# One level of Strassen's seven half-size products for the second product of each feed-forward sublayer

## The chip, the cores and the metric

The kernel runs on one core of a Trainium2 chip. The metric is the device time of one execution in microseconds. TensorE (PE) multiplies matrices and writes PSUM, of which this kernel uses eight banks of 128 x 512 float32; VectorE (DVE) and ScalarE (ACT) work elementwise between PSUM and the on-chip memory SBUF; SyncE (SP) issues the DMA transfers from the chip's main memory.

## The reference

Two layers, each of three sublayers: a half-step SwiGLU feed-forward, a token mixer (mLSTM in the first layer, Mamba-2 in the second), and another feed-forward. There are 512 tokens, 1024 model columns and 2816 feed-forward columns, all float32. So the feed-forward occurs four times:

```python
def swiglu(h, w1, w3, w2):
    return (jax.nn.silu(h @ w1) * (h @ w3)) @ w2

def sublayer(x, fn, g_pre, g_post, shift, scale, gate, weight):
    hmod = rms_norm(x, g_pre) * (1 + scale[:, None, :]) + shift[:, None, :]
    y = rms_norm(fn(hmod), g_post)
    return x + weight * gate[:, None, :] * y
```

The shift, scale and gate rows come from a product of the conditioning vector with the weights `ada_w` (adaLN). The change touches the product with `w2`: 512 x 2816 by 2816 x 1024.

## The kernel before

Every large product is made from split operands: a value becomes a high part in the type fp32r (a ScalarE copy) and a low part (VectorE: value minus high part). `mm3` (L171 to L175) then issues three matmuls for one block: high by high, high by low, low by high. Weights come through `unit` (L146): one 512 KB load into one of four `raw` buffers, a ScalarE copy to `wh` (L161) and a VectorE subtraction to `wl` (L162), three buffers each.

A feed-forward sublayer (`Ffn`) runs in two stages. In the first, `tile_in` makes 22 tiles `f` of 128 feed-forward columns by 512 tokens: two projections of 24 matmuls (w1, w3) into two of four rotating `mm` banks, Silu on ScalarE, the multiply on VectorE (L585), and a split into the halves `gh` and `gl`, which are kept for all 22 tiles. Between tiles `pump` adds steps of the adaLN product of later sublayers: a 512 KB load and a VectorE multiply-add (L195) each, and at the end of each such product a few small matmuls into an `aux` bank. The first four tiles are made in two halves of 256 tokens (`first`), since the second half of the tokens is normalised later.

In the second stage `out_proj` multiplies the tokens (stationary, 128 at a time) by blocks of `w2` (moving, 512 columns). The left half of the model columns is made first into four `aux` banks, then the right half into four `mm` banks; for the last five weight units of the right half, `out_tail` holds the weights and finishes one 128-token tile after another. For each finished bank `Post.evac` squares (ScalarE, L444) and multiplies by the gate row (VectorE, L445); `Post.finish` computes the norm and updates `x`, and `Pre.tok` and `Pre.half` normalise and transpose the tokens for the next sublayer, two 128-token tiles at a time, into eight chunks `hm` (L345 to L347).

SBUF tiles come from pools and from 52 numbered slots; a tile program orders the instructions of each engine ahead of time by priority, in which the program's order counts, and `tc.high_priority()` moves the split of weights up.

## Time and profile before

| | before |
|---|---|
| median of 3 runs | 2109.82 us (2108.58 to 2111.18) |
| the profiled execution | 2108.79 us, of which the profile's span is 2107.0 |
| TensorE busy | 2080.6 us, 99% of the span, 10686 matmuls |
| VectorE busy | 1256.6 us, 60% |
| ScalarE busy | 863.6 us, 41% |
| moved by DMA | 288.32 MB, 137 GB/s on average |

Busy times are shares of an average over stages. Matmuls are pipelined, so the durations of single matmuls overlap and their spacing in the timeline is what counts.

### The profile page before, as it was taken

What the parts mean: (1) busy time and instruction counts of PE and PEld (TensorE: products, weight loads), DVE (VectorE), ACT (ScalarE), POOL (GpSimd) and SP (SyncE); (2) the same over time, 40 slices, a digit from 0 to 9 for tenths busy, and PEclk for the clock granted to TensorE, in tenths of its full rate; (3) what the DMA queues carried; (4) which work ended last, traced back from release to release, by engine and by line L of the source; (5) the groups of instructions that cost most, each with busy time, mean ns of one, the idle gap of its engine ahead of it and who ended that gap; (6) DMA issues with size and microseconds to landing.
All of it is one profiled execution on the core that took longest, in us unless ns stands there. A gap on an engine that the chain in (4) does not pass through costs nothing.

```text
span 2107.0 us, 27076 instructions
## 1 busy us (share of the span) xinstructions
PE 2080.6 (99%) x10686; PEld 1749.8 (83%) x10686; DVE 1256.6 (60%) x1935; ACT 863.6 (41%) x1401; POOL 12.6 (1%) x33
## 2 busy tenths in 40 slices
PE   7999999999999999999999999999999999999998
PEld 5888888988789888888988888898788789888887
DVE  8977524658886667236565423679898865333333
ACT  5433323545463333235332223554656645222231
POOL 0000000000000000000000000000000000000000
PEclk9999999999999999999999999999999999999999
DMA  7566534145325776342565234233434332333331
GB/s 273 189 210 220 189 99 141 51 136 174 122 88 183 230 238 222 99 128 92 171 219 181 90 100 128 93 95 104 140 99 128 110 100 81 100 92 99 100 102 59
DMA packets 89966, 288.32 MB, mean 137 GB/s; under 512 B 11432, under 2 KB 11432, under 8 KB 89840
## 3 DMA queue, kind: packets, MB, share of 16 engines
q1 hardware_dynamic: 89840, 286.61, 42.6%
q8 instruction: 83, 1.36, 0.3%
q14 instruction: 43, 0.35, 0.0%
HBM read 284.32 MB, written 2.24 MB: 136 GB/s over the span
## 4 chain that ended last, share of the span: by engine, by line
PE 93%; DVE 3%; ACT 2%; DMA 1%; issue 1%; SPq 0%; DVEq 0%; ACTq 0%
PE mm L173 25%; PE mm L175 25%; PE mm L174 25%; PE aux L173 4%; PE aux L174 4%; PE aux L175 4%; PE aux L332 1%; PE aux L976 1%; PE aux L753 1%; DMA raw<-in_ada_w 1%; DVE wl L162 1%; PE aux L987 1%; PE aux L941 1%; PE aux L739 0%; ACT wh L161 0%
## 5 line engine op out<-in xcount | busy, mean ns | idle before, releaser
L173 PE MATMUL mm<-hm,wh 128*128 128x512 f32 (+1 forms) x2128 | 770.9, 364 | 1.2 <-ACT hm L417 1.1
L175 PE MATMUL mm<-hm,wl 128*128 128x512 f32 (+1 forms) x2128 | 768.7, 362 | 0.0
L174 PE MATMUL mm<-hm,wh 128*128 128x512 f32 (+1 forms) x2128 | 768.3, 362 | 0.0
L161 ACT ACTIVATE wh<-raw 128x1024 fp32r<-128x1024 f32 (+1 forms) x402 | 373.1, 943 | 740.2 <-PE mm L174 268.5
L162 DVE TENSOR_TENSOR wl<-raw,wh 128x1024 fp32r<-128x1024 f32 (+1 forms) x402 | 428.5, 1078 | 400.7 <-ACT wh L161 392.3
L173 PEld LDWEIGHTS mm<-hm,wh 128*128 128x128 f32 x2128 | 400.9, 189 | 63.4 <-issue 2.1
L175 PEld LDWEIGHTS mm<-hm,wl 128*128 128x128 f32 x2128 | 402.0, 189 | 61.8 <-issue 1.1
L174 PEld LDWEIGHTS mm<-hm,wh 128*128 128x128 f32 x2128 | 401.9, 189 | 60.5 <-issue 1.4
L195 DVE SCALAR_TENSOR_TENSOR acc<-raw,csil,acc 128x1024 f32<-128x1024 f32 x112 | 143.7, 1283 | 143.4 <-DMA raw<-in_ada_w 142.7
L585 DVE TENSOR_TENSOR s<-s,mm 128x512 f32<-128x512 f32 (+1 forms) x97 | 59.9, 618 | 134.4 <-PE mm L175 134.3
L173 PE MATMUL mm<-wh,gh 128*128 128x512 f32 x352 | 137.5, 391 | 0.0
L175 PE MATMUL mm<-wh,gl 128*128 128x512 f32 x352 | 137.0, 389 | 0.0
L174 PE MATMUL mm<-wl,gh 128*128 128x512 f32 x352 | 137.0, 389 | 0.0
L173 PE MATMUL aux<-wh,gh 128*128 128x512 f32 x352 | 136.9, 389 | 0.0
L174 PE MATMUL aux<-wl,gh 128*128 128x512 f32 x352 | 136.9, 389 | 0.0
L175 PE MATMUL aux<-wh,gl 128*128 128x512 f32 x352 | 136.9, 389 | 0.0
L178 ACT ACTIVATE gh<-s 128x512 fp32r<-128x512 f32 (+1 forms) x100 | 57.8, 580 | 121.6 <-DVE s L585 112.9
L175 PEld LDWEIGHTS mm<-wh,gl 128*128 128x128 f32 x352 | 66.1, 188 | 13.9
L175 PEld LDWEIGHTS aux<-wh,gl 128*128 128x128 f32 x352 | 66.1, 188 | 13.8
L173 PEld LDWEIGHTS aux<-wh,gh 128*128 128x128 f32 x352 | 66.1, 188 | 13.8
L174 PEld LDWEIGHTS aux<-wl,gh 128*128 128x128 f32 x352 | 66.1, 188 | 13.6
L173 PEld LDWEIGHTS mm<-wh,gh 128*128 128x128 f32 x352 | 66.1, 188 | 13.5
(261 smaller groups left out, 2113.9 us busy)
## 6 DMA issues: line engine op xcount, KB each, us to landing
raw<-in_w SPq DMA_DIRECT2D x258, 512.0 KB, 3.7
raw<-in_ada_w SPq DMA_DIRECT2D x128, 512.0 KB, 4.3
raw<-in_mb_wx SPq DMA_DIRECT2D x24, 512.0 KB, 3.7
a<-in_ada SPq DMA_DIRECT2D x32, 256.0 KB, 5.4
raw<-in_mb_wz SPq DMA_DIRECT2D x16, 512.0 KB, 3.7
bc<-mb_a SPq DMA_DIRECT2D x32, 256.0 KB, 3.4
raw<-in_mb_wout SPq DMA_DIRECT2D x16, 512.0 KB, 3.7
raw<-in_ml_wkq SPq DMA_DIRECT2D x8, 512.0 KB, 3.7
```

Of the source, the lines that this page charges most:

```text
L161: act(hi[:, :b - a], raw[:, a:b], AF.Copy)
L162: tt(lo[:, :b - a], raw[:, a:b], hi[:, :b - a].bitcast(F32), ALU.subtract)
L173: matmul(ps, stat[0], mov[0], start=first, stop=False)
L174: matmul(ps, stat[0], mov[1], start=False, stop=False)
L175: matmul(ps, stat[1], mov[0], start=False, stop=last)
L178: act(dst_h, src, AF.Copy)
L195: stt(st["acc"], raw, csil[:, kc:kc + 1], st["acc"], ALU.mult, ALU.add)
L332: nc.tensor.transpose(self.pt[d // 2][:, o:o + P], scr[:, d * P:(d + 1) * P], ident)
L585: tt(s[:, a:b], s[:, a:b], p[1][:, a:b], ALU.mult)
L753: matmul(num[j][:, c * P:], vt[c // 2][:, o:o + P], st[c][:, c * P:], start=c == 0, stop=c == 3)
L941: matmul(ps, bt[:, c * P:(c + 1) * P], w, start=True, stop=True)
L976: return matmul(yp[e * 64:(e + 1) * 64, c * P:(c + 1) * P], xdt[c][:, hh * 64:(hh + 1) * 64], ws[e][:, c * P:(c + 1) * P], start=True, sto ...
```

## The change

The product with `w2` is cut into two by two blocks: tokens in halves of 256, the 22 feed-forward tiles in pairs (even, odd), model columns in halves of 512. Seven products of sums and differences of these blocks take the place of eight. `factors` makes the token side of a pair: sums on VectorE, then splits; three factors (products 1, 6, 7) live in buffers of the pool `yg` and are used at once, four (products 2 to 5) are kept in slots. `flush` loads both column halves of the pair's weights, adds them up, splits, and multiplies products 1, 7 and 6 between the tiles of the first stage. They accumulate in all four `aux` banks and two `mm` banks, so that the tiles of the first stage have two `mm` banks (`mm_turn`), and adaLN's small matmuls take a matmul bank where no other is free (`ps_ada`). In `outp`, products 5, 3, 4 and 2 follow, each with loads of its own; product 2 runs with product 4 for four of the 11 pairs, and for the other seven (`HELD`) from held weights at the end, one 128-token tile after another. The output blocks are sums of the seven, made in `yg` on VectorE; the first two token tiles are finished after product 4, the other two after product 2.

```diff
-W2_TAIL = 5
+HELD = 7
...
-    mm = pool("mm", 4, space=bass.MemoryType.PSUM)
+    mm = pool("mm", space=bass.MemoryType.PSUM)
...
-    def ps_mm():
-        return mm.tile([P, T], F32, tag="mm", name="mm")
+    mm_turn, mm_next = [0, 1, 2, 3], [0]
+    def ps_mm(k=None):
+        if k is None:
+            k = mm_turn[mm_next[0] % len(mm_turn)]
+            mm_next[0] += 1
+        return mm.tile([P, T], F32, tag=f"mm{k}", name="mm")
     def ps_aux():
         return banks.get(F32, "aux")
     done_ps = banks.free
+    def ps_ada():
+        if banks.free_:
+            ps = ps_aux()
+            return ps, lambda: done_ps(ps)
+        return ps_mm(), lambda: None
...
-            ps = ps_aux()
+            ps, done = ps_ada()
...
-            done_ps(ps)
+            done()
...
-    def pump(n):
-        settle()
+    def pump(n, ended=True):
+        if ended:
+            settle()
...
     class Ffn:
         def __init__(self, l, h):
-            self.l, self.h, self.s = l, h, 2 * h
-            self.g, self.w, self.raw = {}, {}, {}
+            self.l, self.h, self.sub = l, h, 2 * h
+            self.w, self.raw, self.s, self.half = {}, {}, {}, {}
+            self.kept, self.pairs, self.pending, self.m, self.n_done = {}, [], [], None, 0
         def weights(self, f, hold=False):
             self.w[f] = [unit(i["w13"][self.l, self.h, f, q], hold=hold, soon=not hold) for q in range(2)]
@@ -565,29 +580,111 @@
             if q == 0:
                 act(s0, s0, AF.Silu, bias=b)
                 return
-            self.g[f] = gh, gl = slot(F32R, "gh"), slot(F32R, "gl")
             stt(s0, s1, b, s0, ALU.add, ALU.mult)
-            split(gh, gl, s0)
-            free(s0, s1)
-
-        def tile_in(self, f, sl, hm, p=None):
+            free(s1)
+            self.gated(f, s0)
+        def tile_in(self, f, sl, hm, p=None, go=True):
             a, b = sl
             if f not in self.w:
                 self.weights(f)
             p = p or [ps_mm(), ps_mm()]
             for q in range(2):
                 proj(p[q], self.w[f][q], hm, sl)
-            if f not in self.g:
-                self.g[f] = (slot(F32R, "gh"), slot(F32R, "gl"))
-            gh, gl = self.g[f]
-            s = slot(name="s")
+            if f not in self.half:
+                self.half[f] = slot(name="s")
+            s = self.half[f]
             act(s[:, a:b], p[0][:, a:b], AF.Silu)
             tt(s[:, a:b], s[:, a:b], p[1][:, a:b], ALU.mult)
-            split(gh[:, a:b], gl[:, a:b], s[:, a:b])
-            free(s)
             if b == T:
                 for w in self.w[f]:
                     free(*w.tiles)
+                del self.half[f]
+                self.gated(f, s)
+                if go:
+                    self.step()
+        def gated(self, f, s):
+            self.s[f] = s
+            if f ^ 1 in self.s:
+                self.pairs.append(f // 2)
+        def step(self):
+            self.flush()
+            if self.pairs:
+                self.factors(self.pairs.pop(0))
+        def factors(self, j):
+            s0, s1 = self.s.pop(2 * j), self.s.pop(2 * j + 1)
+            H = T // 2
+            lo, hi = slice(0, H), slice(H, T)
+            raw = ygp.tile([P, D], F32, tag="yg", name="traw")
+            tt(raw[:, :T], s0, s1, ALU.add)
+            tt(raw[:, T:T + H], s0[:, lo], s1[:, hi], ALU.add)
+            tt(s0[:, hi], s0[:, hi], s0[:, lo], ALU.subtract)
+            tt(s1[:, lo], s1[:, lo], s1[:, hi], ALU.subtract)
+            th = ygp.tile([P, D], F32R, tag="yg", name="th")
+            tl = ygp.tile([P, D], F32R, tag="yg", name="tl")
+            early = {}
+            for n, (m, src) in enumerate(((1, raw[:, T:T + H]), (6, s0[:, hi]), (7, s1[:, lo]))):
+                c = slice(n * H, n * H + H)
+                split(th[:, c], tl[:, c], src)
+                early[m] = th[:, c], tl[:, c]
+            self.kept[j] = kept = {}
+            for (ma, a), (mb, b) in (((5, raw[:, lo]), (3, s0[:, lo])), ((2, raw[:, hi]), (4, s1[:, hi]))):
+                kh, kl = slot(F32R, "kh"), slot(F32R, "kl")
+                split(kh[:, lo], kl[:, lo], a)
+                split(kh[:, hi], kl[:, hi], b)
+                kept[ma], kept[mb] = (kh[:, lo], kl[:, lo]), (kh[:, hi], kl[:, hi])
+                kept[f"{ma}{mb}"] = kh, kl
+            free(s0, s1)
+            self.pending.append((j, early))
+        def product(self, ps, a, b, first, last):
+            for t in range(2):
+                c = slice(t * P, (t + 1) * P)
+                mm3(ps[t], (a[0][:, c], a[1][:, c]), b, first, last)
+        def w2(self, c, j):
+            raw = rawp.tile([P, 1024], F32, tag="raw", name="raw")
+            nc.sync.dma_start(raw, i["w2"][self.l, self.h, c, j])
+            return raw
+        def halves(self, raw, n=2 * T):
+            wh = whp.tile([P, 1024], F32R, tag="wh", name="wh")
+            wl = wlp.tile([P, 1024], F32R, tag="wl", name="wl")
+            split(wh[:, :n], wl[:, :n], raw[:, :n])
+            return [(wh[:, k * T:k * T + T], wl[:, k * T:k * T + T]) for k in range(n // T)]
+        def flush(self):
+            while self.pending:
+                j, a = self.pending.pop(0)
+                if self.m is None:
+                    self.m = {1: [ps_aux(), ps_aux()], 6: [ps_aux(), ps_aux()], 7: [ps_mm(2), ps_mm(3)]}
+                settle()
+                r0, r1 = self.w2(0, j), self.w2(1, j)
+                with tc.high_priority():
+                    tt(r1[:, :T], r1[:, :T], r0[:, :T], ALU.add)
+                    two = r0.rearrange("p (a b) -> p a b", b=T)
+                    tt(two, two, r1[:, T:].unsqueeze(1).to_broadcast([P, 2, T]), ALU.add)
+                    b1, b7 = self.halves(r0)
+                    b6, = self.halves(r1, T)
+                n = self.n_done
+                self.n_done += 1
+                for m, b in ((1, b1), (7, b7), (6, b6)):
+                    self.product(self.m[m], a[m], b, n == 0, n == NF // 2 - 1)
         def first(self, hm):
             for f in range(F_STAG):
@@ -595,16 +692,99 @@
             for f in range(F_STAG):
                 self.tile_in(f, HA, hm)
             for f in range(F_STAG):
-                self.tile_in(f, HB, hm)
+                self.tile_in(f, HB, hm, go=False)
+            mm_turn[:] = [0, 1]
         def rest(self, hm, start, rate):
             for f in range(start, NF):
                 self.tile_in(f, FULL, hm)
                 if f < ADA_END:
-                    pump(int((f - start + 1) * rate) - int((f - start) * rate))
-
-        def outp(self, post):
-            out_proj(i["w2"][self.l, self.h], [self.g[f] for f in range(NF)], W2_TAIL, post)
+                    pump(int((f - start + 1) * rate) - int((f - start) * rate), False)
+        def outp(self, nxt):
+            n = NF // 2
+            m5 = [ps_mm(0), ps_mm(1)]
+            def five(j):
+                raw = rawp.tile([P, 1024], F32, tag="raw", name="raw")
+                nc.sync.dma_start(raw[:, :T], i["w2"][self.l, self.h, 1, j, :, T:])
+                with tc.high_priority():
+                    b5, = self.halves(raw, T)
+                self.product(m5, self.kept[j][5], b5, j == 0, j == n - 1)
+            for j in range(n - 2):
+                five(j)
+            while self.pairs or self.pending:
+                self.step()
+            post = Post(self.l, self.sub, nxt)
+            m, yg = self.m, post.yg
+            lo, hi = slice(0, T), slice(T, D)
+            for t in range(2):
+                act(yg[2 + t][:, hi], m[1][t], AF.Copy)
+                tt(yg[t][:, lo], yg[2 + t][:, hi], m[7][t], ALU.add)
+                tt(yg[2 + t][:, hi], yg[2 + t][:, hi], m[6][t], ALU.add)
+            done_ps(*m[1], *m[6])
+            for j in range(n - 2, n):
+                five(j)
+            m3 = [ps_aux(), ps_aux()]
+            for j in range(n):
+                raw = self.w2(1, j)
+                with tc.high_priority():
+                    tt(raw[:, lo], raw[:, lo], raw[:, hi], ALU.subtract)
+                    b3, = self.halves(raw, T)
+                self.product(m3, self.kept[j][3], b3, j == 0, j == n - 1)
+                free(*self.kept[j]["53"])
+            for t in range(2):
+                act(yg[t][:, hi], m5[t], AF.Copy)
+                tt(yg[t][:, lo], yg[t][:, lo], m5[t], ALU.subtract)
+                tt(yg[t][:, hi], yg[t][:, hi], m3[t], ALU.add)
+                tt(yg[2 + t][:, hi], yg[2 + t][:, hi], m3[t], ALU.add)
+                post.evac(t, 1, yg[t][:, hi])
+            done_ps(*m3)
+            m4, m2 = [ps_aux(), ps_aux()], [ps_mm(2), ps_mm(3)]
+            held = {}
+            joint = range(3, 3 + 2 * (n - HELD), 2)
+            hs = [j for j in range(n) if j not in joint]
+            for j in range(n):
+                raw = self.w2(0, j)
+                k = self.kept[j]
+                if j in joint:
+                    with tc.high_priority():
+                        tt(raw[:, hi], raw[:, hi], raw[:, lo], ALU.subtract)
+                        b2, b4 = self.halves(raw)
+                    self.product(m4, k[4], b4, j == 0, j == n - 1)
+                    self.product(m2, k[2], b2, j == joint[0], False)
+                    free(*k["24"])
+                    continue
+                tt(raw[:, hi], raw[:, hi], raw[:, lo], ALU.subtract)
+                b4 = slot(F32R, "bh"), slot(F32R, "bl")
+                split(*b4, raw[:, hi])
+                held[j] = slot(F32R, "bh"), slot(F32R, "bl")
+                split(*held[j], raw[:, lo])
+                self.product(m4, k[4], b4, j == 0, j == n - 1)
+                free(*b4)
+            for t in range(2):
+                tt(yg[t][:, lo], yg[t][:, lo], m4[t], ALU.add)
+                act(yg[2 + t][:, lo], m4[t], AF.Copy)
+            done_ps(*m4)
+            for t in range(2):
+                post.evac(t, 0, yg[t][:, lo])
+                post.finish(t)
+            for t in range(2):
+                c = slice(t * P, (t + 1) * P)
+                for j in hs:
+                    ah, al = self.kept[j][2]
+                    mm3(m2[t], (ah[:, c], al[:, c]), held[j], False, j == hs[-1])
+                    if t:
+                        free(*self.kept[j]["24"], *held[j])
+                u = 2 + t
+                tt(yg[u][:, lo], yg[u][:, lo], m2[t], ALU.add)
+                post.evac(u, 0, yg[u][:, lo])
+                tt(yg[u][:, hi], yg[u][:, hi], m2[t], ALU.subtract)
+                post.evac(u, 1, yg[u][:, hi])
+                post.finish(u)
+            mm_turn[:] = [0, 1, 2, 3]
+            return post
...
     for f in range(3, START_L + 6):
-        f00.tile_in(f, FULL, p.hm)
+        f00.tile_in(f, FULL, p.hm, go=False)
         k = f - START_L
         if k >= 0:
             f00.late(k // 2, k % 2, early[k // 2][k % 2])
         pump(START_R[f - 3])
     done_ps(mod0)
+    mm_turn[:] = [0, 1]
     f00.rest(p.hm, START_L + 6, ADA_R[0])
-    post = Post(0, 0, (0, 1))
-    f00.outp(post)
+    post = f00.outp((0, 1))
...
-    post = Post(0, 2, (1, 0))
-    f01.outp(post)
+    post = f01.outp((1, 0))
...
-    f11.outp(Post(1, 2))
+    f11.outp(None)
```

## Rows read from the trace of the kernel before

**Rows 1.** The page's head: span, and busy time (share of the span) by engine.

```profile
span 2107.0 us, 27076 instructions
PE 2080.6 (99%) x10686; PEld 1749.8 (83%) x10686; DVE 1256.6 (60%) x1935; ACT 863.6 (41%) x1401; POOL 12.6 (1%) x33
```

**Rows 2.** The chain of work that ended last, shares of the span by engine.

```profile
PE 93%; DVE 3%; ACT 2%; DMA 1%; issue 1%; SPq 0%; DVEq 0%; ACTq 0%
```

**Rows 3.** Waits: engine, line, releaser: us in total, times, longest.

```profile
DVE acc L195 <- DMA raw<-in_ada_w: 142.7, 65, 5.1
...
PE aux L410 <- DVE diag L392: 12.3, 4, 9.8
PE aux L941 <- DVE xw L938: 1.3, 1, 1.3
```

**Rows 4.** Groups of instructions by line and shape: count, busy us, mean ns.

```profile
L162 DVE TENSOR_TENSOR wl<-raw,wh 128x1024 fp32r<-128x1024 f32 x294 | 359.1, 1222 | 393.0 <-ACT wh L161 389.2 <-DMA bc<-mb_a 2.0 <-PE aux L914 0.6
...
L173 PE MATMUL aux<-wh,gh 128*128 128x512 f32 x352 | 136.9, 389 | 0.0
...
L161 ACT ACTIVATE wh<-raw 128x512 fp32r<-128x512 f32 x108 | 63.6, 630 | 14.1 <-DMA raw<-in_w 7.6 <-PE mm L174 3.1 <-DVE ss L311 0.8
```

**Rows 5.** Timeline of TensorE, two stretches: start us, duration us, instruction.

```profile
261.69 0.39 PE L173 MATMUL mm<-hm,wh 128*128 128x512 f32 x1
...
272.34 0.39 PE L175 MATMUL mm<-hm,wl 128*128 128x512 f32 x1
...
988.43 0.28 PE L173 MATMUL mm<-hm,wh 128*128 128x256 f32 x1
...
991.54 0.28 PE L175 MATMUL mm<-hm,wl 128*128 128x256 f32 x1
```

**Rows 6.** Windows: stretch, busy us (count) by engine, granted clock, DMA share, GB/s.

```profile
0.00:30.00 30.00, 15.85 (x61) 12.45 (x62) 20.73 (x72) 20.23 (x35) 2.00 (x9) 1.00 0.92 333
...
90.00:155.00 65.00, 65.00 (x292) 53.84 (x291) 48.24 (x69) 22.75 (x30) 0.00 (x0) 1.00 0.69 212
155.00:285.00 130.00, 130.00 (x616) 107.46 (x615) 75.23 (x83) 41.30 (x51) 0.00 (x0) 1.00 0.56 187
285.00:340.00 55.00, 55.00 (x244) 45.53 (x243) 15.55 (x15) 13.85 (x20) 0.00 (x0) 1.00 0.31 96
...
640.00:870.00 230.00, 230.00 (x1202) 194.51 (x1201) 146.30 (x168) 75.20 (x102) 0.00 (x0) 1.00 0.62 202
...
1770.00:1990.00 220.00, 220.00 (x1027) 184.55 (x1027) 71.10 (x79) 59.84 (x79) 0.00 (x0) 1.00 0.29 90
...
2045.00:2107.00 62.00, 54.58 (x241) 44.86 (x239) 21.35 (x41) 13.83 (x26) 0.00 (x0) 0.98 0.20 68
```

**Rows 7.** Timeline of VectorE at the crossing to the second sublayer, idle before in brackets.

```profile
379.57 0.69 DVE L445 TENSOR_TENSOR yg<-mm,grow 128x512 f32<-128x512 f32 x1 [0.29 <-ACT sq L444]
380.18 0.20 DVE L295 TENSOR_SCALAR rc<-ssq 128x1 f32<-128x1 f32 x1
...
383.80 0.15 DVE L297 TENSOR_SCALAR rc<-st 128x1 f32<-128x1 f32 x1 [1.22 <-ACT yg L325]
...
384.88 0.75 DVE L327 TENSOR_SCALAR yg<-x,rc 128x1024 f32<-128x1024 f32 x1
...
404.97 1.45 DVE L345 TENSOR_SCALAR hv<-aux,mod,mod 128x256 f32<-128x256 f32 x3 [0.53 <-PE aux L332]
...
411.31 0.43 DVE L347 TENSOR_TENSOR hm<-hv,hm 128x256 fp32r<-128x256 f32 x1 [0.63 <-ACT hm L346]
```

**Rows 8.** DMA issues: tensors, count, KB each, median us from issue to landing.

```profile
raw<-in_w SPq DMA_DIRECT2D x258, 512.0 KB, 3.7
...
a<-in_ada SPq DMA_DIRECT2D x32, 256.0 KB, 5.4
```

**Rows 9.** Timeline behind the last matmul, all engines.

```profile
2099.62 0.60 ACT L444 ACTIVATE sq<-mm 128x512 f32<-128x512 f32 x1 [4.94 <-PE mm L175]
...
2102.07 1.41 DVE L455 SCALAR_TENSOR_TENSOR x<-yg,rc,x 128x512 f32<-128x512 f32 x2
```

7 lines of the change are left out of this document (3 added, 4 removed).

## Prediction

> **What bounds the kernel now.** I read the page's head first: TensorE is busy for 2080.6 of 2107.0 us, VectorE 60%, ScalarE 41% [rows 1]. A busy TensorE need not be a full one, so next came the chain of work that ended last: 93% of it is TensorE, and no other engine has more than 3% [rows 2]. Then the list of waits: the longest wait of TensorE is 12.3 us, all at the opening, and the next is 1.3 us [rows 3]. So the time is the number of matmuls times their spacing. The durations of the grouped lines (389 ns, [rows 4]) overlap and are not that spacing; the timeline is. From 261.69 to 272.34 us lie 47 steps of 512-column matmuls, 10.65 us, 0.2266 us each; from 988.43 to 991.54 lie 26 steps of 256 columns, 0.120 us each [rows 5]. Last I read the windows by stage, because the change spends VectorE and DMA time to save TensorE time: VectorE is busy for 74% of 90 to 155 us, 58% of 155 to 285, 64% of 640 to 870 and 32% of 1770 to 1990 [rows 6]. It has room on average, not everywhere. TensorE's granted clock is 1.00 in these windows, and 0.98 in the last of all, where TensorE stands idle for 7.4 us [rows 6]; so I price idle time as itself.
>
> **What is removed.** The second product of a sublayer is 22 blocks of the contraction by 4 token tiles by 2 column halves by 3 terms (high by high, high by low, low by high): 528 matmuls. After it, seven products of 11 pairs by 2 token tiles by 3 terms: 462, of the same 512 columns and the same 128x128 stationary side. That is 66 fewer per sublayer, 264 in four, and 264 x 0.2266 = 59.8 us of TensorE time.
>
> One rule speaks against so much: the Trainium skill, TensorE: Matmul & The Clock Gate, section Back-to-back issue gap, gives some 131 ns for a 512-column matmul in a real stream of weight loads and matmuls. By it the gain would be an estimated 264 x 0.131 = 34.6 us. The trace differs, 226.6 ns over 47 steps [rows 5], and the trace decides.
>
> **What is added on VectorE.** Prices: a 512-column operation starts 0.61 us before the next (379.57 to 380.18, [rows 7]), a 1024-column one takes 1.22 us [rows 4], a 256-column one I put at 0.35, between half of 0.61 and the 0.43 of the row at 411.31 [rows 7]. For a pair of first-product tiles: one 512-column and three 256-column sums, seven 256-column low halves, 0.61 + 10 x 0.35 = 4.1 us, in place of two low halves, 1.2 us. For its first three products' weights: sums of 512 and 1024 columns and low halves of the same, 0.61 + 1.22 + 1.22 + 0.61 = 3.7 us. So 6.6 us more for each pair, in a stretch that grows by 18 matmuls, 4.1 us.
>
> **The stage of first products.** A pair of tiles is 96 matmuls, 21.8 us, and becomes 25.8. VectorE goes from 58% to (12.6 + 6.6)/25.8 = 74% in the middle of the first sublayer, to 79% in the second, 53% in the last [rows 6]. The tight place is the first sublayer near 90 to 155 us: four pairs were put off and are made one per tile, so VectorE needs 0.74 x 10.9 + 6.6 = 14.7 of 15.0 us. There the sublayer has only two PSUM banks for its tiles, where it had four: TensorE reaches a bank again one projection (24 matmuls, 5.4 us) after its last matmul, where it was three, 16.3 us. VectorE's multiply must be done in that time. I take 3 us of stall in all, most in the first sublayer; the ends are 0 and, with 0.5 us for each of VectorE's 65 waits for adaLN weights [rows 3], 32 us.
>
> **The stage after the first products.** TensorE has 18 matmuls of the last pair, 66 for the fifth product, 66 for the third, 66 for the fourth and 24 for the part of the second that runs with it: 240, 54.4 us; then 42 for the rest of the second, 9.5 us. VectorE has, up to the same point: last pair 4.1 and 3.7; fifth product's low halves 11 x 0.61 = 6.7; four sums of the first evacuation, 2.4; third product 22 x 0.61 = 13.4; eight operations of the next evacuation, 4.9; fourth and second 4 x (0.61 + 1.22) + 7 x 3 x 0.61 = 20.1. Sum 55.3 us against 54.4: balanced, where this stage had VectorE busy for 15.6 of 55 us [rows 6]. The loads come on top. In the third product 512 KB feed six matmuls, 1.36 us. Each of four raw buffers is held for the landing (3.7 us, [rows 8]), a sum 0.61, a ScalarE copy 0.63 [rows 4], a low half 0.61 and some 0.5 us of handing over: 6.05 us, one block per 1.51 us, 0.15 over, 11 times: 1.7 us. With the 0.9 us of VectorE's sum I take 2.5 us per sublayer, 10 us for four. Ends: 0, if the fifth product's slack puts blocks ahead; 15 us per sublayer with the opening's landing of 5.4 us (rival D).
>
> The loads' rate points the same way: at the opening 333 GB/s flowed with the DMA 92% busy [rows 6], and at that rate 512 KB take 1.57 us, not 1.36. The Trainium skill, DMA: Bandwidth & Descriptors, section Specifications, puts HBM's limit for a core at about 358 GB/s; by it a block would take an estimated 1.46 us, and the third product would lose 11 x 0.10 = 1.1 us per sublayer in place of my 1.7. The trace's 333 GB/s lies under that limit, as it must.
>
> **The crossing to the next sublayer.** Before, the four token tiles end 6.8 us apart, and after the second one TensorE still has two tiles, 13.6 us, before it needs the next sublayer's first half of tokens. After, the first two tiles end together, with 9.5 us of matmuls and some 1.7 us of transposes behind them: 11.2 us. VectorE needs eleven instructions per tile, 4.3 us of work (379.57 to the one at 384.88, [rows 7]); two tiles and the two new sums of 0.61 make 9.9. With 1.5 us of ScalarE waits that the other tile can't fill (one alone is 1.22 in the row at 383.80), a transposing burst and 0.5 us to VectorE, the first normalised chunk stands at about 13.3 us: a gap of 2.1. Its eight chunks then come 0.84 us apart (404.97 to 411.74, [rows 7]); two open banks take 6 x 0.120 = 0.72 us of matmuls each, another 1 us or so. I take 3.5 us, three times: 10.5 us. Ends: 0, and 10 if nothing runs before the last chunk (13.3 + 8 x 0.84 less 11.2 is 8.8). The third and fourth tile are covered by the first half's matmuls, four tiles or 23 us.
>
> **The end.** After the last matmul stands a square, a product, a norm and the last update (2099.62 to 2103.48, [rows 9]). Now a sum (0.61) comes first and a second square and product go between (about 1.1): 1.7 us more, with nothing to cover it.
>
> Moving the sums and the ScalarE copies of the banks costs nothing where ScalarE has its 59% idle; adaLN's banks being taken from the matmul banks is covered by the 18 matmuls that follow them (4.1 us), and without these it costs about 1 us for each of some thirty.
>
> **The sum.** The profiled execution took 2108.8 us, 1.0 below the median shown, inside the spread of the runs. 2108.8 - 59.8 + 3 + 10 + 10.5 + 1.7 = 2074.2. I forecast 2074 us.
>
> **Rivals.**
> A, the forecast: part of the gain goes back at the crossings and in the balanced stage; own range 2062 to 2090. Chance 0.55.
> B, all stalls are filled, since the instruction order already sets transposes between matmuls (no crossing shows a wait of TensorE over 1.3 us, [rows 3]): 2108.8 - 59.8 + 1.7 and 5 us of rest give 2056. VectorE's 55.3 us against 54.4 speaks against it. Chance 0.20.
> C, two banks don't cover VectorE's lateness in the tiles with adaLN work: 65 x 0.5 = 32 us in place of 3, so 2103. For it: waits up to 5.1 us stand in VectorE's in-order queue [rows 3], against 5.4 us of cover. Against it: those waits fall where VectorE has nothing older to do. Chance 0.16, a quarter of it within 0.2%.
> D, slower: the ring of four raw buffers becomes the bound of the whole second stage. With a landing of 5.4 us, as at the opening [rows 8], a block of the fifth product takes 1.8 us (against 1.36), of the third 1.94, of the fourth and second 2.25 (against 1.86): 11 x (0.42 + 0.58 + 0.39) = 15.3 us per sublayer, 61 in all, and 2108.8 - 59.8 + 61 + 15 = 2125. It decides from (59.8 - 15.2)/4 = 11.2 us per sublayer, 0.34 us for each of 33 blocks. For it: each block carries half the matmuls that a 512 KB load fed before. Against it: this stage holds no adaLN loads, and loads of this tensor land in 3.7 us. Chance 0.09.
>
> **How the numbers follow.** The time is A's. Below 2055 only the full gain without B's rest lies, about 1 in 20; above 2102 lie D and a third of C, about 0.15. So the range is 2055 to 2102. A measurement tells this kernel from no change beyond 0.2%, 4 us: faster 0.55 + 0.20 + 0.12 = 0.87, same 0.04, slower 0.09.
>
> **What would show it.** 264 fewer matmuls at a spacing still near 0.227 us; TensorE idle of some 25 us more, in four short stretches behind the first products and at three crossings, ended by the low halves of weights and by normalised chunks. VectorE above 90% between the third product and the end of the fourth. C would show as waits of the next tile's projection for the multiply, D as ScalarE or VectorE waiting for raw loads. The forecast is wrong if the spacing grows, since then the count of matmuls is no longer the price, or if the idle time lies in the stage of first products.

## The result, and the profile after

| | before | after |
|---|---|---|
| median, runs side by side | 2110.5 us (2108.58 to 2111.57, 4 runs) | 2160.26 us (2158.57 to 2164.35, 4 runs) |
| the profiled execution | 2108.79 us | 2159.1 us, span 2157.1 |
| matmuls | 10686 | 10422 |
| TensorE busy | 2080.6 us | 2061.5 us |

The ratio is 1.024, 95% interval [1.0222, 1.0257]: the kernel is slower by 50 us where 2074 us, faster by 36, was forecast. The busy times from the page's head, the chain and the row of the DMA issues for the same loads, after:

```profile
PE 2061.5 (96%) x10422; PEld 1709.9 (79%) x10422; DVE 1625.5 (75%) x2699; ACT 1004.8 (47%) x1769; POOL 12.5 (1%) x33
...
PE 67%; DVE 15%; DMA 11%; ACT 4%; issue 3%; DVEq 0%; ACTq 0%; SPq 0%
...
raw<-in_w SPq DMA_DIRECT2D x346, 512.0 KB, 4.3
```

The 264 matmuls are gone, as counted, but TensorE's busy time falls by 19.1 us, not by 59.8, and the chain that was 93% TensorE [rows 2] is 67% TensorE, 15% VectorE and 11% DMA: the kernel is no longer bound by the number of matmuls alone. The waits say on what it stands besides (us in total, times, longest):

```profile
PE aux L346 <- DVE yg L341: 19.5, 6, 5.3
PE mm L186 <- ACT wh L191: 13.5, 4, 3.8
...
PE aux L186 <- ACT wh L191: 11.8, 7, 2.8
PE aux L187 <- DVE wl L192: 7.8, 17, 1.1
PE mm L252 <- DVE s L598: 3.9, 2, 3.0
```

The opening's row of `diag`, 12.2 us, is as before [rows 3]. These are new: transposes at the crossings that wait for a normalised tile (19.5), products that wait for the halves of their weights (13.5 at the first joint block of products 4 and 2; 11.8, of which 10.5 at the last pair; 7.8, most in the third product), gate rows of adaLN that wait for a matmul bank (3.9). The windows show where and at what clock (columns as in [rows 6]):

```profile
320.00:425.00 105.00, 88.68 (x429) 72.02 (x428) 88.45 (x167) 58.44 (x111) 0.00 (x0) 0.92 0.54 180
425.00:940.00 515.00, 506.40 (x2751) 427.05 (x2751) 389.97 (x569) 229.51 (x386) 8.54 (x17) 1.00 0.53 170
940.00:1035.00 95.00, 79.69 (x368) 64.00 (x367) 82.39 (x152) 55.50 (x103) 0.00 (x0) 0.89 0.57 187
...
1322.00:1425.00 103.00, 86.27 (x418) 69.80 (x417) 87.95 (x166) 58.44 (x111) 0.00 (x0) 0.90 0.55 184
...
2080.00:2157.20 77.20, 57.67 (x232) 42.74 (x230) 62.06 (x105) 32.87 (x60) 0.00 (x0) 0.93 0.54 179
```

TensorE idles in the four stretches that hold the stages behind the first products, 16.3, 15.3, 16.7 and 19.5 us, and in these the granted clock is under 1.00; in the long stretches between it is 1.00. The last stretch has the end of the kernel in it. TensorE's timeline shows the two things together, at the last pair, at the first joint block of products 4 and 2, and at the crossing to the second sublayer:

```profile
327.46 0.39 PE L188 MATMUL mm<-wh,kl 128*128 128x512 f32 x1
330.36 0.80 PE L186 MATMUL aux<-wh,th 128*128 128x512 f32 x2 [2.51 <-ACT wh L191]
...
332.67 0.63 PE L187 MATMUL aux<-wl,th 128*128 128x512 f32 x1
333.09 0.63 PE L188 MATMUL aux<-wh,tl 128*128 128x512 f32 x1
...
334.81 0.40 PE L187 MATMUL mm<-wl,th 128*128 128x512 f32 x1
335.04 0.39 PE L188 MATMUL mm<-wh,tl 128*128 128x512 f32 x1
...
360.68 0.39 PE L188 MATMUL aux<-bh,kl 128*128 128x512 f32 x1
364.26 0.73 PE L186 MATMUL mm<-wh,kh 128*128 128x512 f32 x2 [3.20 <-ACT wh L191]
...
385.38 0.39 PE L188 MATMUL aux<-bh,kl 128*128 128x512 f32 x1
...
394.90 0.39 PE L188 MATMUL mm<-bh,kl 128*128 128x512 f32 x1
...
402.61 1.97 PE L346 MATMUL aux<-ident,yg 128*128 128x128 f32 x8 [4.92 <-DVE yg L341]
405.44 0.80 PE L186 MATMUL mm<-hm,wh 128*128 128x256 f32 x2 [0.86 <-ACT hm L360]
```

After 2.51 us of idle the matmuls stand 0.42 us apart (332.67 to 333.09), and at 334.81 to 335.04 again 0.23: the clock at its lower level for some matmuls, then back. So this stall cost more than its idle time.

Against what the terms of the prediction need, the loss lies like this. TensorE's timeline cuts each sublayer's second part in two: from the first matmul of the fifth product to the end of product 4, for which the prediction has 54.4 us, the trace has 70.4 (315.2 to 385.6), 70.5, 69.9 and 69.1. From there to the first matmul of the next sublayer the prediction has 9.5 + 1.7 = 11.2 us, the trace 19.8 (385.6 to 405.4), 19.7 and 20.8; in the last sublayer, which has no crossing, the 9.5 us are 9.5.

| | predicted loss | measured loss |
|---|---|---|
| stages of first products, mixers included | 3 | 1.7 + 9.5 + 6.1 + 1.2 = 18.5 |
| behind the first products, to the end of product 4 | 10 | 16.0 + 16.1 + 15.5 + 14.7 = 62.3 |
| crossings | 10.5 | 8.6 + 8.5 + 9.6 = 26.7 |
| end | 1.7 | 2.8 |
| sum | 25.2 | 110.3 |

By the times the sum is 2159.1 - (2108.8 - 59.8) = 110.1 us; the rest is rounding. In the largest row no engine is full. The first 70.4 us (columns as in [rows 6]):

```profile
315.20:385.60 70.40, 61.16 (x241) 46.00 (x240) 57.74 (x89) 33.74 (x56) 0.00 (x0) 0.95 0.69 228
```

VectorE is busy for 57.7 us, near the 55.3 of the prediction's sum, and idle for 12.7; so its total doesn't set the length of this stage.

### The profile page after: what moved, and what is told of

Same layout as the page of the kernel before. It is cut to its first block, busy times and chain, and to the rows that moved or that the text cites. A ratio compares the mean times of both kernels' runs of the same rounds, so it can differ in the third digit from the quotient of the medians.

```text
span 2157.1 us, 28206 instructions
## 1 busy us (share of the span) xinstructions
PE 2061.5 (96%) x10422; PEld 1709.9 (79%) x10422; DVE 1625.5 (75%) x2699; ACT 1004.8 (47%) x1769; POOL 12.5 (1%) x33
## 4 chain that ended last, share of the span: by engine, by line
PE 67%; DVE 15%; DMA 11%; ACT 4%; issue 3%; DVEq 0%; ACTq 0%; SPq 0%
PE mm L186 19%; PE mm L188 19%; PE mm L187 19%; DMA raw<-in_w 8%; DMA raw<-in_ada_w 2%; DVE wl L192 2%; PE aux L186 2%; DVE wl L175 2%; PE aux L187 2%; PE aux L188 2%; DVE acc L208 2%; ACT wh L174 1%; ACT wh L191 1%; PE aux L1156 1%; DVE raw L681 1%
## 5 line engine op out<-in xcount | busy, mean ns | idle before, releaser
L174 ACT ACTIVATE wh<-raw 128x1024 fp32r<-128x1024 f32 (+1 forms) x294 | 278.8, 957 | 409.1 <-PE mm L187 131.9
L175 DVE TENSOR_TENSOR wl<-raw,wh 128x1024 fp32r<-128x1024 f32 (+1 forms) x294 | 320.5, 1096 | 118.5 <-ACT wh L174 114.8
L191 ACT ACTIVATE wh<-raw 128x1024 fp32r<-128x1024 f32 (+1 forms) x192 | 145.3, 763 | 299.0 <-PE mm L187 127.8
L192 DVE TENSOR_TENSOR wl<-raw,wh 128x1024 fp32r<-128x1024 f32 (+1 forms) x192 | 162.9, 854 | 48.8 <-ACT wh L191 46.5
L186 PE MATMUL aux<-wh,th 128*128 128x512 f32 x176 | 70.0, 406 | 10.5 <-ACT wh L191 10.5
L187 PE MATMUL aux<-wl,th 128*128 128x512 f32 x176 | 69.6, 396 | 0.0
L188 PE MATMUL aux<-wh,tl 128*128 128x512 f32 x176 | 69.5, 395 | 0.0
L597 ACT ACTIVATE s<-mm 128x512 f32<-128x512 f32 (+1 forms) x97 | 51.3, 531 | 23.2 <-PE mm L188 23.2
L186 PE MATMUL mm<-wh,kh 128*128 128x512 f32 x120 | 48.1, 409 | 13.5 <-ACT wh L191 13.5
L187 PE MATMUL aux<-wl,kh 128*128 128x512 f32 x120 | 50.2, 418 | 9.3 <-DVE wl L192 7.8
L681 DVE TENSOR_TENSOR raw<-raw 128x1024 f32<-128x1024 f32 x44 | 53.8, 1222 | 1.1
L1049 DVE SCALAR_TENSOR_TENSOR cv<-mm,c_mb_cw,cv 128x511 f32<-128x511 f32 (+2 forms) x72 | 53.3, 742 | 0.6
```

Source lines behind the costliest of these rows:

```text
L174: act(hi[:, :b - a], raw[:, a:b], AF.Copy)
L175: tt(lo[:, :b - a], raw[:, a:b], hi[:, :b - a].bitcast(F32), ALU.subtract)
L186: matmul(ps, stat[0], mov[0], start=first, stop=False)
L187: matmul(ps, stat[0], mov[1], start=False, stop=False)
L188: matmul(ps, stat[1], mov[0], start=False, stop=last)
L191: act(dst_h, src, AF.Copy)
```

## The experiments

Theory L: the loads and splits of weights come late behind the first products. Theory Q: at the crossings work stands in the wrong order in VectorE's and ScalarE's in-order queues. Theory C: the lower clock behind each stall is the larger part. Theory V: VectorE's added operations. Theory H: too little cover at the crossings. The last column gives the stretch from the first matmul of the fifth product to the first of the next sublayer (in the last sublayer, to its last matmul), in the four feed-forward sublayers in order, from TensorE's timeline of the one profiled execution. The kernel before ran beside each group of runs, with medians from 2109.9 to 2111.9 us; so 2 us between groups say nothing.

| run | median us | ratio to before, interval | stretch, us |
|---|---|---|---|
| the changed kernel | 2160.3 | 1.024 [1.0222, 1.0257] | 90.3, 90.2, 90.7, 78.4 |
| e1_no_loads | 2123.6 | 1.0071 [1.0054, 1.0088] | 83.0, 80.2, 80.2, 70.8 |
| e2_five_buffers | 2154.6 | 1.0211 [1.0196, 1.0227] | 90.7, 86.7, 86.5, 74.2 |
| e3_zero_matmuls | 2182.8 | 1.0341 [1.0326, 1.0357] | 96.8, 95.2, 94.8, 85.5 |
| e4_shared_loads | 2131.8 | 1.0103 [1.0088, 1.0118] | 84.6, 82.7, 83.3, 69.9 |
| e5_order | 2163.4 | 1.0244 [1.0219, 1.0269] | 86.9, 87.9, 90.5, 78.2 |
| e6_held_nine | 2166.6 | 1.0267 [1.0251, 1.0283] | 93.2, 90.6, 92.4, 80.8 |
| e7_together | 2134.1 | 1.0109 [1.0094, 1.0124] | 79.0, 82.3, 82.1, 69.8 |
| e8_no_sums | 2149.1 | 1.0188 [1.017, 1.0207] | 86.5, 87.9, 87.5, 75.1 |
| e9_chain | 2121.1 | 1.005 [1.0026, 1.0073] | 77.4, 77.6, 77.4, 73.2 |
| e9_chain_alone | 2153.2 | 1.0205 [1.0186, 1.0225] | 85.8, 85.3, 84.6, 79.8 |
| e10_chain_nine | 2119.9 | 1.0038 [1.0024, 1.0052] | 78.8, 75.9, 77.9, 69.5 |
| e11_all | 2128.5 | 1.0083 [1.0069, 1.0097] | 80.4, 75.3, 74.4, 70.1 |
| e12_two_banks (the kernel before, edited) | 2165.0 | 1.0254 [1.0228, 1.0279] | none |
| e13_no_weight_sums | 2149.3 | 1.0182 [1.0165, 1.0199] | 88.2, 87.5, 87.6, 77.4 |

### e1_no_loads: are the loads late?

```diff
         def w2(self, c, j):
+            if self.fixed:
+                self.fixed.append(self.fixed.pop(0))
+                return self.fixed[-1]
...
+            self.fixed = [self.w2(1, j) for j in range(4)]
```

> The changed kernel with the loads behind the first products left out: four w2 blocks are loaded once at the start of that stage and used in turn by the last pair's products and by products 5, 3, 4 and 2, so the output is not the reference's. VectorE's and ScalarE's work is the same. Theory L (the short ring of four load buffers: each block feeds only six matmuls, 1.36 us, and a load takes 4 us and more): most of the idle time of TensorE between the first products and the end of product 4 goes, about 13 us per sublayer with the slow clock behind it, so about 2105 us. Theory V (VectorE's 55 us of work bind that stage): no load is missing where TensorE waits, so 2150 to 2160 us.

Measured: 2123.6, 37 us less, two thirds of what theory L wanted. TensorE's waits:

```profile
PE aux L187 <- DVE bl L192: 9.5, 4, 2.4
PE aux L186 <- ACT bh L191: 3.9, 4, 1.3
```

The waits for `wh` (13.5 and 11.8) and `wl` (7.8) are gone from the list. What stays is no load: 19.2 us at the crossings, and 13.4 us in four places where product 4 begins, for halves that VectorE and ScalarE make behind the sums of the evacuation between products 3 and 4. That is as long as the wait of the joint blocks was, at the same place: with no load to wait for, the sums hold TensorE up (the first low half that it waits for, at 353.28 in this run, stands behind seven of the eight operations). To the end of product 4 the stretches are now 61.5, 60.6, 60.5 and 61.5 us, 8 to 10 less. The loads are about a third of the 110 us.

### e2_five_buffers: is the ring of four the reason?

```diff
-    rawp = pool("rawp", 4)
+    rawp = pool("rawp", 5)
...
-            self.diag.append(const.tile([P, P], F32, name=f"diag{t}"))
+            self.diag.append(slot(name="diag"))
```

> The changed kernel with five raw buffers in place of four; two small constants move to slots to make the room. Output unchanged. Theory L: a block may take 6.05/5 = 1.21 us instead of 1.51, below the 1.36 of its matmuls, so the third product's gaps go and the last pair's weights come one block earlier: some 6 to 8 us per sublayer, about 2130 us. Theory V: within 5 us of 2160.

Measured: 2154.6, 5.6 us less, not 30. The waits at the joint blocks hardly move (13.5 to 12.8 us), those of the last pair and the third product fall from 11.8 to 7.4, and the wait of the gate rows doubles, 3.9 to 7.6. One more buffer is not the remedy for a load that is issued late: SyncE issues its loads in the program's order, and the last pair's two, at 321.40 and 322.67 in the first sublayer, stand behind those of nine blocks of the fifth product, each of which held a whole buffer for 256 KB.

### e3_zero_matmuls: is it the clock?

Matmuls of zeros are meant to stand where TensorE stalls, so that it has no idle time there: 12 before the last pair, 14 at the first joint block, 28 at each crossing.

```diff
+    def idle(ps, n, first=False):
+        for _ in range(n):
+            matmul(ps, ones_r, zer, start=first, stop=first)
...
+            idle(m5[0], 12)
...
+                    if j == 3:
+                        idle(m4[0], 14)
...
+                with tc.issue_after(end.ins):
+                    idle(ps_mm(0), 28, True)
```

> The changed kernel with matmuls by a tile of zeros where TensorE waited: 12 into a bank of product 5 ahead of the last pair's products, 14 into a bank of product 4 ahead of its first block with product 2, and 28 at each of three crossings into a bank that nobody reads. Output unchanged. They do no work and take the place of idle time. Theory C (the idle time makes the granted clock fall to the lower of its two levels, and the stretches at it cost some 30 of the 110 us lost): granted clock 1.00 until the end and 20 to 30 us less, 2130 to 2140 us. Rival (the idle time is the whole cost and the lower clock falls into it): 2160 us or a few more.

Measured: 2182.8, 22.6 us more. The stretches at the lower clock fall from 70.5 to 44.8 us in all, the tail included, but at the joint block the zeros came behind the wait and not into it:

```profile
364.83 0.79 PE L193 MATMUL mm<-wh,kh 128*128 128x512 f32 x1 [4.29 <-ACT wh L198]
...
372.06 3.38 PE L160 MATMUL aux<-zer,ones_r 128*128 128x512 f32 x14
```

So the wait stayed (17.3 us in four places, 13.5 without the zeros), and 3.2 us of zeros came on top in each sublayer. At the crossings they did fill the wait: the transposes wait 1.9 us in place of 19.5. There the second and third crossing show something: no stretch at the lower clock is left at them (granted clock 1.00 from 1015 to 1040 and from 1405 to 1430 us), and they take 19.6 and 19.8 us from the end of product 4, against 19.7 and 20.8. So, as far as these two show, the lower clock adds about a microsecond at most to the length of a crossing. What it costs at the other places the run doesn't show. What the clock cost is left to the windows: 1 - 0.92, 0.89, 0.90 and 0.93 of 105, 95, 103 and 77.2 us, over the one half that the lower level takes away, are 16.8 + 20.9 + 20.6 + 10.8 = 69 us at 1.2 GHz, idle time among it and the tail of the kernel. What counts of it is the matmuls that ran in it: 151 records start there, with columns worth 20.8 us at the upper level, so they lost at most about as much again.

### e4_shared_loads: fewer, earlier loads

Product 5 takes two pairs from one buffer, and the last three from the load that product 3 makes anyway, so that seven of the 11 buffers of product 5 go, and the last pair's loads stand behind three of them, not nine.

```diff
-            for j in range(n - 2):
-                five(j)
+            for j in range(0, 6, 2):
+                five(j, j + 1)
...
-                    b3, = self.halves(raw, T)
+                    b3, *b5 = self.halves(raw, D if j > 7 else T)
+                if b5:
+                    self.product(m5, self.kept[j][5], b5[0], False, j == n - 1)
...
-            joint = range(3, 3 + 2 * (n - HELD), 2)
+            joint = range(1, 1 + 2 * (n - HELD), 2)
```

> The changed kernel with fewer, fuller loads: product 5 takes two blocks per load buffer for the pairs 0 to 7, and shares product 3's load for the pairs 8 to 10; six blocks of product 5 stand ahead of the last pair's products in place of nine; product 2 runs with product 4 for the pairs 1, 3, 5, 7 in place of 3, 5, 7, 9. Same matmuls, same VectorE work but for fewer, wider instructions. Output unchanged. Theory L: the last pair's loads are issued earlier and three of eleven blocks of product 3 feed twelve matmuls: 4 to 8 us per sublayer, about 2135 us. Theory V: the same work in VectorE, within 5 us of 2160.

The edit also moves the first joint block from the fourth place to the second (`joint`); what of the gain at the joint blocks is loads and what is this order was not parted.

Measured: 2131.8, 28.5 us less with the whole computation. The wait at the crossings:

```profile
PE aux L346 <- DVE yg L341: 25.8, 6, 5.9
```

The waits for weights of products 1 to 7 fall from some 34 us to 14. To the end of product 4 the stretches are 60.3 to 61.0 us, as short as without any loads (e1), and 6 us over the 54.4 are left. The crossings have become longer, 24.3, 22.2 and 22.3 us from the end of product 4 against 19.8, 19.7 and 20.8, so that a part of the gain goes back there.

### e5_order, e6_held_nine, e7_together: the crossing, first tries

```diff
+            second = nxt and post.pre.end
...
+                with tc.issue_after(second.ins) if nxt else nullcontext():
```
```diff
-HELD = 7
+HELD = 9
```

The first diff (e5) sets the sums of the third and fourth tile behind the normalisation of the second; the other (e6) gives the crossing 12 matmuls more of cover; e7 has both, with e2 and e4.

> The changed kernel with one edge of order: VectorE's sums and products for the third and fourth token tile (after product 2) are issued behind the last step of the second token tile's normalisation. Output unchanged. Theory O (the crossing is long because VectorE takes some 4 us of that work, which nobody waits for, between the two tiles that the next sublayer waits for): the 5 us wait between the two bursts of transposes falls to about 1, 4 to 5 us at each of three crossings, about 2147 us. Rival (the chain of the two tiles itself is that long, or its work is only moved to the second half of the tokens, which then comes late): within 4 us of 2160.

> The changed kernel with product 2 held back for nine pairs in place of seven (HELD = 9), so that 54 of its matmuls, 12.2 us, stand behind product 4 in place of 42, 9.5 us. Output unchanged. Theory H (the crossing lacks cover, and the matmuls of product 4 are the bound before it): 2.7 us less at each of three crossings, and nothing at the last: about 2152 us. Rival (the stage of product 4 is bound by VectorE and loads, so that the matmuls moved behind it leave as much idle time there): within 3 us of 2160.

> The shared loads of the fourth run, the order of the fifth, nine held pairs and five raw buffers (with three small constants in slots) in one kernel. Output unchanged. If the shares add up: 2132 from the shared loads, less 12 to 15 from the order, 8 from the held pairs and some 6 from the fifth buffer: 2100 to 2108 us, a little under the kernel before. If VectorE's total work behind the first products is the bound that comes next: 2115 to 2125 us.

Measured: 2163.4, 2166.6 and 2134.1. None helps: e5 takes the transposes' wait from 19.5 to 13.8 us in the profiled run (2154.6, the fastest of its four), and the median doesn't follow; e6 has it at 22.4; e7 is e4 (2131.8) again. So it was neither the sums of the later tiles alone nor want of cover. VectorE's timeline of the changed kernel shows what else stands in the way:

```profile
387.61 0.69 DVE L459 TENSOR_TENSOR yg<-yg,grow 128x512 f32<-128x512 f32 x1 [0.68 <-ACT sq L458]
...
388.70 0.69 DVE L459 TENSOR_TENSOR yg<-yg,grow 128x512 f32<-128x512 f32 x1
...
390.87 1.28 DVE L472 SCALAR_TENSOR_TENSOR x<-yg,rc,x 128x1024 f32<-128x1024 f32 x1
392.07 1.22 DVE L175 TENSOR_TENSOR wl<-raw,wh 128x1024 fp32r<-128x1024 f32 x1
393.21 0.68 DVE L781 TENSOR_TENSOR yg<-yg,mm 128x512 f32<-128x512 f32 x1
...
393.87 0.20 DVE L309 TENSOR_SCALAR rc<-ssq 128x1 f32<-128x1 f32 x1
...
395.80 0.74 DVE L341 TENSOR_SCALAR yg<-x,rc 128x1024 f32<-128x1024 f32 x1
...
401.81 0.74 DVE L341 TENSOR_SCALAR yg<-x,rc 128x1024 f32<-128x1024 f32 x1
```

The second tile has its gate product at 388.70, 1.1 us behind the first one's at 387.61. But its norm starts (`rcol`, L309) at 393.87, behind the first tile's whole update (L472) and two other operations: the next sublayer's weight half (L175) and the third tile's sum (L781). Its normalised tokens come at 401.81, 6.0 us behind the first's.

### e8_no_sums: VectorE's sums between products 3 and 4

```diff
-                tt(yg[t][:, lo], yg[t][:, lo], m5[t], ALU.subtract)
-                tt(yg[t][:, hi], yg[t][:, hi], m3[t], ALU.add)
-                tt(yg[2 + t][:, hi], yg[2 + t][:, hi], m3[t], ALU.add)
-                post.evac(t, 1, yg[t][:, hi])
+                act(yg[t][:, hi], m3[t], AF.Square, accum_out=post.ssq[:, 2 * t + 1:2 * t + 2])
```

> The changed kernel without VectorE's eight operations between products 3 and 4 (the sums with products 5 and 3 and the multiply by the gate row are left out for the blocks made there, so the output is not the reference's; ScalarE's copy and square stay). Loads, matmuls and all else are the same. Theory V at this place (the wait of 3 us and the slow clock behind it at the first block with product 2 come from these 4.9 us of VectorE): that wait goes, 5 to 6 us per sublayer, about 2138 us. Theory L (the load of that block is late): the wait stays, within 6 us of 2160.

Measured: 2149.1, 11 us less, half of what theory V wanted. The wait of the joint blocks is gone, as theory V says (13.5 us in the changed kernel):

```profile
PE mm L186 <- ACT wh L191: 1.5, 3, 1.0
```

The stretches win 2.3 to 3.8 us, about the idle time itself (3.1 to 3.8), not the 5 to 6 with the lower clock behind it. How the sums cost that time is a matter of order. In the changed kernel the joint block itself waited for its load, while two blocks of product 4 that had landed before it stood behind it. ScalarE and VectorE there:

```profile
358.96 0.63 ACT L191 ACTIVATE bh<-raw 128x512 fp32r<-128x512 f32 x1 [0.18 <-DMA raw<-in_w]
...
360.93 0.61 ACT L191 ACTIVATE bh<-raw 128x512 fp32r<-128x512 f32 x1
```
```profile
362.29 0.69 DVE L753 TENSOR_TENSOR raw<-raw 128x512 f32<-128x512 f32 x1 [0.23 <-DMA raw<-in_w]
...
365.39 0.68 DVE L759 TENSOR_TENSOR raw<-raw 128x512 f32<-128x512 f32 x1
```

The second and third block (ScalarE's copies at 358.96 and 360.93) had landed, but VectorE made four sums of the evacuation, then the joint block's difference (L753), for whose load it waited, and theirs (L759) only from 365.39 on; TensorE stood idle until 364.26. L753 waits for its load in the other sublayers too, 0.18 to 0.87 us. In e8 VectorE and TensorE take these two blocks ahead of the joint block, and TensorE doesn't wait for it. With e1, where the wait is as long without any load, the sums are what costs, and the order of the blocks around them.

### e9_chain and e9_chain_alone: the queues in order

Both tiles' norms run side by side, the two updates of `x` follow both norms, and the next sublayer's held weight splits and the sums of the later tiles are issued behind the second tile's square and normalisation.

```diff
+                for e in edge if hold else ():
+                    held.enter_context(tc.issue_after(e.ins))
                 act(hi[:, :b - a], raw[:, a:b], AF.Copy)
...
+                rs = [rcol(post.ssq[:, 2 * t:2 * t + 1], post.ssq[:, 2 * t + 1:2 * t + 2]) for t in range(2)]
+                with tc.issue_after(last_rc[0].ins):
+                    for t in range(2):
+                        stt(x[t], yg[t], rs[t], x[t], ALU.mult, ALU.add)
+                post.pre = Pre(*nxt)
+                for t in range(2):
+                    post.pre.tok(t, yg[t])
+                edge[:] = [post.pre.sq, post.pre.end]
```

> The kernel with shared loads, and at the three crossings another order of the same operations: the norms and updates of the first two token tiles run side by side, and VectorE's and ScalarE's splits of the next sublayer's first held weights, and the sums of the third and fourth token tile, are issued behind the second tile's square and normalisation. Theory Q (at the crossing TensorE waits for work that stands in the two in-order queues ahead of the second tile's norm, not for the chain itself): the 11 us lost at each crossing of the kernel with shared loads fall to some 5 to 7, so 2131.75 less 3 x (4 to 6), 2114 to 2120 us. Rival (the chain from the end of product 4 to the first normalised chunk is too long in itself, whatever stands beside it): within 4 us of 2131.75, and the waits of the transposes for the normalised tiles keep their 10 us.

> The changed kernel with nothing but the other order at the crossings (norms of the first two tiles side by side, the next sublayer's first weight splits and the sums of the third and fourth tile behind them). Theory Q: 9 us lost at each crossing fall to 3 to 5, so 2160 less 3 x (4 to 6), 2142 to 2148 us. Rival (the chain itself is too long): 2156 to 2164.

Measured: 2121.1 and 2153.2: 10.7 and 7.1 us less than without the order, between theory and rival. The row of the transposes and VectorE's timeline, e9_chain:

```profile
PE aux L351 <- DVE yg L346: 9.0, 5, 3.5
```
```profile
390.17 0.75 DVE L346 TENSOR_SCALAR yg<-x,rc 128x1024 f32<-128x1024 f32 x1
...
391.39 0.75 DVE L346 TENSOR_SCALAR yg<-x,rc 128x1024 f32<-128x1024 f32 x1
```

The two normalised tiles are now 1.2 us apart, not 6.0, and 25.8 us of waits became 9.0. From the end of product 4 the crossings take 16.6, 16.1 and 15.2 us, 4.0 to 5.4 over the 11.2 of cover, where e4 had 11.0 to 13.1; in e9_chain_alone 15.1, 15.4 and 14.2, where the changed kernel had 8.5 to 9.6 over. That is theory Q, at the crossing itself. A part of it went back elsewhere in the profiled execution (2126.2, the slowest of five): the last stretch is 3.3 us longer than e4's, and two stages of first products 4.6 us (522.0 to 526.6, 292.4 to 297.1); why is not shown. The 4.0 to 5.4 us that are left speak for the rival in part: the chain itself is longer than its cover.

### e10_chain_nine and e11_all

> The kernel of e9_chain (2121.1 us) with nine pairs of the second product held for the end in place of seven: 12 more matmuls, 2.7 us, between product 4 and each crossing. Theory Q (with the queues in order, the crossing is short of cover only, so more cover now pays, as it did not in e6_held_nine): up to 3 x 2.7 less, 2113 to 2117 us. Rival (nine held pairs leave only two joint blocks, and the wait that is taken from the crossing comes back at the blocks of product 4 that run alone): 2119 to 2126.

> The kernel of e10_chain_nine with a fifth raw buffer and loads of products 5 that serve two pairs at once. Theory L with Q (what is left in the stage behind the first products is half late loads and half crossings): another 4 to 8 us below e10_chain_nine, 2106 to 2112 us, level with the kernel before at 2110. Rival (loads have no part left once products 5 and 3 share theirs): within 3 us of e10_chain_nine.

Measured: 2119.9 and 2128.5. More cover wins nothing beyond the spread of e9_chain (2113.4 to 2126.2), and the waits for the blocks of product 4 that run alone rise from 1.1 to 5.5 us, as the rival has it. The fifth buffer costs 8.6 us here, though two of its stretches are the shortest of all: its stages of first products are longer, and the gate rows' wait is 6.3 us against 3.1. In all three kernels with a fifth buffer that wait rose (7.6, 6.6, 6.3); why was not settled. e10_chain_nine is the best version found, 1.0038 [1.0024, 1.0052]: the product by Strassen comes to within 0.4% of the kernel before and doesn't beat it.

### e12_two_banks and e13_no_weight_sums: the stages of first products

The kernel before gets the change's bank rule alone (e12); the changed kernel loses the sums in `flush` (e13). In these two runs theory C is that the two banks cost the time, and rival V that VectorE's added work does.

```diff
+    def ps_ada():
+        if len(mm_turn) == 4:
+            ps = ps_aux()
+            return ps, lambda: done_ps(ps)
+        return ps_mm(), lambda: None
...
         def rest(self, hm, start, rate):
+            mm_turn[:] = [0, 1]
```
```diff
-                    tt(r1[:, :T], r1[:, :T], r0[:, :T], ALU.add)
-                    two = r0.rearrange("p (a b) -> p a b", b=T)
-                    tt(two, two, r1[:, T:].unsqueeze(1).to_broadcast([P, 2, T]), ALU.add)
```

> The kernel before with one part of the change alone: from the first full tile to the end of the first products of each feed-forward sublayer its tiles have two matmul banks in place of four, and adaLN's small matmuls take one of these two. Theory C (the two banks cost the 15 us that the changed kernel lost in the stages of first products): 2120 to 2126 us. Rival V (VectorE's added sums and low halves cost them, and two banks alone are covered): 2109 to 2113, no change.

> The changed kernel without the two sums of weights in flush (one of 512 and one of 1024 columns on VectorE, 1.8 us for each of 44 pairs); products 1, 6 and 7 then take unsummed blocks of w2, so the output is not the reference's. Matmuls, loads and banks stay. Rival V (VectorE's added work costs the time in the stages of first products): 8 to 12 us less than 2160, 2148 to 2152, and the waits of the projections for low halves of weights go. Theory C (the banks do): within 4 us of 2160, but for the first 2 us of each stage behind them.

Measured, e12: 2165.0, 53 us more than before, where even theory C wanted 10 to 14. The stages of first products grow by 15.7, 21.8 and 14.8 us, and by 0.2 in the last sublayer, which has no adaLN work. Waits, and TensorE's timeline at two of them:

```profile
PE mm L183 <- DVE s L595: 19.1, 9, 4.2
PE mm L249 <- DVE s L595: 13.1, 6, 4.5
```
```profile
154.20 0.80 PE L249 MATMUL mm<-adah,ones_r 128*128 128x512 f32 x1 [3.89 <-DVE s L595]
...
189.86 0.75 PE L226 MATMUL mm<-ones_b,adas 128*128 128x1 bf16 x24
194.81 0.80 PE L183 MATMUL mm<-hm,wh 128*128 128x512 f32 x1 [4.20 <-DVE s L595]
195.41 0.63 PE L184 MATMUL mm<-hm,wh 128*128 128x512 f32 x1
195.83 0.63 PE L185 MATMUL mm<-hm,wl 128*128 128x512 f32 x1
```

The gate rows come in twos: the second takes the bank of the tile just done and waits for its multiply (13.1 us). The shift and scale products (L226) come singly and take the other bank, so that the next projection needs the bank of the tile just done and waits for the same multiply (19.1). That makes 32.2 us in all, and the matmuls behind stand 0.42 to 0.43 us apart. In the changed kernel the waits of the gate rows are 3.9 us, and no projection has such a wait: 18 matmuls of a pair stand between. The last sublayer has the same two banks and no small products, and grows by 0.2. So it is two banks with adaLN's small products in them that would eat nearly the whole gain, and products 1, 6 and 7 hide most of it.

Measured, e13: 2149.3, 11 us less, and nearly all of it behind the first products (stretches shorter by 2.1, 2.7, 3.1, 1.0). The stages of first products stay: 523.0 and 522.2 us between the first two stretches, 294.2 and 294.0 between the next. Theory V named the number and not the place, and falls for these stages. What went is the wait of the last pair, 11.8 us in the changed kernel (together with the third product):

```profile
PE aux L186 <- ACT wh L191: 2.5, 6, 0.8
```

The wait of the joint blocks rises at the same time, 13.5 to 19.0 us. So the last pair's 2.5 us of idle have two parts, as the changed kernel's VectorE shows: a load that comes late, and the sums behind it.

```profile
327.13 0.69 DVE L679 TENSOR_TENSOR raw<-raw 128x512 f32<-128x512 f32 x1 [1.96 <-DMA raw<-in_w]
327.86 1.22 DVE L681 TENSOR_TENSOR raw<-raw 128x1024 f32<-128x1024 f32 x1
```

Of the 18.5 us lost in the stages of first products the rows name some 7.5 (3.9 for the bank, 3.2 for low halves, 0.4 for high halves beyond the 1.1 that stood there before); the rest is not settled.

## Why the prediction was wrong

Its step on what is removed held: 264 matmuls fewer, 0.227 us apart in the timeline wherever TensorE doesn't stall; the Trainium skill's 131 ns (TensorE: Matmul & The Clock Gate, Back-to-back issue gap) doesn't show in this kernel's stream. The 59.8 us were there to be won. It gave back 110 where the sum had 25.

**The stage after the first products**, "I take 2.5 us per sublayer", is the first step that failed, and the largest: 14.7 to 16.1 us. The sizes held (VectorE 57.7 us busy where the sum had 55.3, TensorE 54.4); that balanced totals mean little stall did not. Stalls came from the order of the work and from late loads, in three places. The last pair's loads stand in SyncE's queue behind those of nine blocks of the fifth product, and sums of weights stand behind the loads (2.5 to 2.8 us of idle). In the third product each block is up to a microsecond late. The first joint block waits for its load while two landed blocks stand behind it and VectorE makes the sums of the evacuation (3.1 to 3.8 us). The sum had 1.7 us for the third product's loads and 0.9 us of work for VectorE; for the two single waits and the lower clock behind them it had nothing. e1 and e4 (37 and 28.5 us) show the loads; e8 and e13 (11 each) show VectorE's part in the two single waits.

Rival D had the mechanism, late raw loads: 512 KB took 4.3 us to land in the middle, not 3.7, and 5.3 in the third product of the first sublayer, near D's 5.4. Its 15.3 us per sublayer come near the measured loss by luck: they were to lie evenly on 33 blocks, and the waits are two single ones of some 3 us and some 2 us in the third product; and a fifth buffer, which should have cured a short ring, won 5.6 us.

**The crossing**, "I take 3.5 us, three times": 8.5 to 9.6 us each. The cover of 11.2 us was right. The chain was put at 13.3 us to the first normalised chunk, as eleven instructions of two tiles that fill each other's waits; from the end of product 4 (385.6) to the next sublayer's first matmul, which needs that chunk, it took 19.8 us, since the second tile's norm was queued behind the first's update, weight halves of the next sublayer and sums of later tiles. e9 shows what of it is the order: the medians fall by 10.7 and 7.1 us, and the waits of the transposes from 25.8 to 9.0.

**"So I price idle time as itself"** failed: in the four stretches with the stalls the granted clock fell to 0.89 to 0.93. The rows of before had shown it at 0.98 where TensorE idled for 7.4 us. How much of the 110 us this is by itself stays open: idle time is 69 of them (95.6 less 26.4, span less busy), and of the 41 left the matmuls at the lower level are at most some 21.

**The stage of first products**, "I take 3 us of stall": 18.5, mixers included, of which 11 stay without a cause. Rival C's mechanism shows in e12, where two banks don't cover the late multiply, but not in the changed kernel, where the rows have 3.9 us of it. The sentence on adaLN's small matmuls held in kind: covered by the 18 behind a pair, 3.9 us; without these 32.2 us of waits, over 20 products in matmul banks and not thirty, and 53 us with the lower clock behind them.

**The end**, 1.7 us, came to 2.8. VectorE above 90% at the end of the fourth product came true: 23.37 of 25.0 us from 361 to 386.
